# GpSimd's 128x512 tensor instructions of the mixing stages, issued as four of 128x128

## The chip, the cores and the metric

The kernel runs on one core of one Trainium2 chip. The metric is the device time of one execution in microseconds. Five engines of the core work side by side, each through its own instructions in order: TensorE (PE in the profile, with its weight loads as PEld), VectorE (DVE), ScalarE (ACT), GpSimd (POOL) and SyncE (SP), which here only issues DMAs. They wait for one another through semaphores.

## The reference: what is computed

A decoder trunk of two layers on a sequence of 512 positions with 1024 features, in float32. Each layer norms its input, projects it to the columns of three groups of heads, mixes them over the sequence, projects the mixture back, and adds a squared-ReLU MLP:

```python
for l in range(DEPTH):                                   # 2 layers
    h = rms_norm(x, norm_mix_g[l])
    p_att, p_conv, p_rwkv = jnp.split(h @ w_in[l], ...)
    o_att = diff_attention(...)      # 6 heads, causal
    o_conv = short_conv(...)         # 4 groups
    o_rwkv = rwkv7_time_mix(...)     # 6 heads, a recurrence over the sequence
    x = x + jnp.concatenate([o_att, o_conv, o_rwkv], axis=-1) @ w_out[l]
    h = rms_norm(x, norm_mlp_g[l])
    x = x + jnp.square(jax.nn.relu(h @ w_mlp_up[l])) @ w_mlp_down[l]
return rms_norm(x, final_norm_g)
```

## The kernel before, in words

Everything is held transposed: features on the 128 partitions, the 512 positions along the free axis, so that most tiles are 128x512. Each layer has a **mixing stage** (in the profiled execution about 16 to 298 us and 634 to 960 us) and an **MLP stage** (298 to 634 us and 960 to 1263 us).

A float32 product on TensorE is made of three passes: an operand is split into a rounded part (`whi`, `ahi`) and the rest (`wlo`, `alo`), and whi·ahi, whi·alo and wlo·ahi are added up in PSUM. Weights come in halves of four 128x128 tiles: SyncE loads `raw` (128x512, 256 KB), ScalarE casts it to `whi` (L687), and VectorE or GpSimd forms `wlo = raw - whi` (L699). A string of letters, `LO`, says for each half which of the two does it; `rests(dve)` and `rests(pool)` go through the list, and 62 of the halves are GpSimd's. There are three buffers each of `raw`, `whi` and `wlo`. `passes` then issues the three matmuls of one 128x128 weight tile, the wlo pass last.

In the mixing stage nothing is scheduled by a planner. Every job is a Python generator that yields after each instruction: `loads`, `casts`, `rests`, `products` (the projections `pj`, the output projection `po`, and the first three column groups of the MLP's up projection, `up`), `squares` and `inner_norm` (the MLP's norm), `rwkv_pair` and `rwkv_inverse` for each of three pairs of heads, `att_pair`, `conv` and others. A string `ORDER` of letters and counts, one string per layer, says which generator goes on next; `drive` walks through it. So the order in which each engine meets its instructions is written out by hand, and an engine that waits holds everything behind it.

GpSimd's 128x512 tensor instructions in the mixing stages are these, with their lines in the kernel before:

- L699 `wlo`, the rest of a weight half (62 times).
- L769 `accf`, the sum of the squares of x for the MLP's norm, in `norm_steps_of`, called by `squares` (7 per layer). Each adds `sqf`, ScalarE's square of one 128x512 tile of x (L766), to the sum; after the last, `inner_norm` has TensorE sum it over the partitions: four matmuls `pssf`, one per 128 positions (L290 is the helper that issues every matmul). On VectorE, `alof` (L756, in `inputs`) is formed at the same time for `up`.
- L942 `k`, L946 `bb` and L951 `bk` (once per pair of heads): three products in a row in `rwkv_pair`. `bk` and VectorE's `ar` (L950, L952) are the operands of the matmuls `pg`.
- L1016 the rest of a split operand, `pd..lo` (6 times in its several names).
- L1144 `nm` in `rwkv_inverse`: a masked copy, which VectorE reduces to `nd` (L1146). A DMA out and in turns it round, GpSimd inverts small triangles with 30 instructions of 64 partitions (L1158, L1160) and the result `xb` goes out and in by DMA (`dm` L1162, `xd` L1164) to VectorE's L1167 to L1186, and on to the matmuls `px`.
- L1184 `ee`, the other operand of `px`.
- L1248 `cz` and L1255 `cy` in `conv` (4 each).

Together they are 120 instructions. Three things on VectorE stand beside them: its own halves of `wlo` (L699), the operand rests `klo` and `qlo` of attention (L1273), and in `att_pair` the step from softmax sums to weights: `sm` (L1337, 128x1), then `pp` (L1339), then TensorE's transposes `ptt`.

GpSimd also has 128x512 subtractions `ml` in the MLP stages (L1405, 64 of them), a few 128x256 ones (L547), and instructions of the first norm (L400, L455); the change leaves them as they are.

Of the kernel before, what the change touches and what calls it, by code (L numbers as in the profile page):

```python
# [10 lines left out]
F32 = mybir.dt.float32  # L11
# [5 lines left out]
ALU = mybir.AluOpType  # L17
# [6 lines left out]
P = 128  # L24
NK = D // P
NB = S // P
C = 64
# [253 lines left out]
def tile_trunk(ctx: ExitStack, tc: tile.TileContext, xT, wts, prm_d, cst_d, lora_d, gup_d, lam_d, fin_d, out):  # L281
    nc = tc.nc
    act, dve, pool = nc.scalar, nc.vector, nc.gpsimd
# [44 lines left out]
    act.activation(cp.tile([P, NB], F32, tag="rr", bufs=2, name="rr0")[:, :1], ones1, AF.Sqrt)  # L328

    WB = 3  # L330
    lean = [False]

    def weights(g, k0=0, k1=NK, home=None):

        for a in range(k0, k1, 4):
            n = min(4, k1 - a)
            raw = wp.tile([P, 4, P], F32, tag="raw", bufs=WB, name=f"raw{g}_{a}")
            nc.sync.dma_start(raw[:, :n].rearrange("p k c -> p (k c)"), wts[g, :, a * P:(a + n) * P])
            if home is None:
                hi, lo = [wp.tile([P, 4, P], F32R, tag="w" + p, bufs=WB, name=f"w{p}{g}_{a}") for p in ("hi", "lo")]  # L340
            else:
# [47 lines left out]
    nrm = {}  # L389
# [198 lines left out]
    for l in range(L):  # L588
# [3 lines left out]
        key = f"m{l}"  # L592
        lean[0] = True
        with ExitStack() as mx:
# [37 lines left out]
            def loads():  # L632
# [8 lines left out]
                for kind, *o in order:  # L641
                    if kind == "w":
                        g, a, _, k0, k1 = o
                        if k0 == 0:
                            whole[g, a] = wp.tile([P, 4, P], F32, tag="raw", bufs=WB, name=f"raw{wbase + g}_{a}")
                        raw = raws[g, a, k0] = whole[g, a]
# [42 lines left out]
            def rests(which):  # L689
                whole = {}  # L690
                for i, (g, a, n, k0, k1) in enumerate(pieces):
                    eng = dve if g in head or LO[l][i - len(first)] == "x" else pool
                    if eng is which:
                        raw = yield from got(raws, (g, a, k0))
                        hi = yield from got(his, (g, a, k0))
                        if k0 == 0:
                            whole[g, a] = wtile(g, a, 1)
                        lo = los[g, a, k0] = whole[g, a]
                        yield eng.tensor_tensor(lo[:, k0:k1], raw[:, k0:k1], hi[:, k0:k1].bitcast(F32), ALU.subtract)  # L699

            def passes(out_ps, g, k, operand, first, last):
                at = piece(g, k)
# [55 lines left out]
            def norm_steps_of(j, key):  # L758

                if j == 0:  # L760
                    acc = wp.tile([P, S], F32, tag="acc", bufs=1, name=f"acc{key}")
                    nrm[key] = [acc]
                    yield act.activation(acc, x[j], AF.Square)
                else:
                    sq = wp.tile([P, S], F32, tag="sq", bufs=2, name=f"sq{key}_{j}")
                    yield act.activation(sq, x[j], AF.Square)  # L766
                    if j == NK - 1:
                        nrm["all" + key] = True
                    yield pool.tensor_tensor(nrm[key][0], nrm[key][0], sq, ALU.add)  # L769

            def inner_norm():
                key = f"f{l}"
# [122 lines left out]
            c3 = lambda ap: ap.rearrange("p (c s) -> p c s", s=C)  # L895
# [11 lines left out]
            m16 = cst[:, K_M16:K_M16 + C]  # L907
            B = 16

            def rwkv_pair(t):  # L910
                n = f"{l}_{t}"
                zk, zr = tmp(f"zk{t}"), tmp(f"zr{t}")
# [3 lines left out]
                sq = tmp(f"ksq{t}")  # L916
# [13 lines left out]
                w = yield from got(lw, t)  # L930
                dx = mp.tile([P, NCH, C + 1], F32, tag="dx", name=f"dx{n}")
                di = tmp(f"di{t}")
# [5 lines left out]
                a = yield from got(av, t)  # L938
                t1 = tmp(f"t1{t}")
                yield act.activation(t1, a, AF.Identity, scale=pr[:, C_KA + t:C_KA + t + 1], bias=dr[:, 11 + t:12 + t])  # L940
                k2 = tmp(f"k2{t}")
                yield pool.tensor_tensor(k2, zk, t1, ALU.mult)  # L942
                kkn = tmp(f"kkn{t}")
                yield act.activation(kkn, zk, AF.Identity, scale=kcol)
                bb = tmp(f"bb{t}")
                yield pool.tensor_tensor(bb, kkn, a, ALU.mult)  # L946

                ar = mp.tile([P, 2, NCH, C], F32, tag="ar", name=f"ar{n}")
                bk = mp.tile([P, 2, NCH, C], F32, tag="bk", name=f"bk{n}")
                yield dve.scalar_tensor_tensor(ar[:, 0], c3(kkn), -1.0, dx[:, :, :C], ALU.mult, ALU.mult)  # L950
                yield pool.tensor_tensor(bk[:, 0], c3(bb), c3(di), ALU.mult)  # L951
                yield dve.tensor_tensor(ar[:, 1], c3(zr), dx[:, :, 1:], ALU.mult)  # L952
                yield dve.tensor_tensor(bk[:, 1], c3(k2), c3(di), ALU.mult)

# [1 line left out]
                nn = mp.tile([P, 2 * NB, C], F32, tag="nn", name=f"nn{n}")  # L956
# [54 lines left out]
                pd = tmp(f"pd{t}")  # L1011
                yield dve.scalar_tensor_tensor(pd, zr, pr[:, C_RK + t:C_RK + t + 1], k2, ALU.mult, ALU.mult)
                phi = mp.tile([P, S], F32R, tag="ty", bufs=2, name=f"pd{n}hi")
                yield act.copy(phi, pd)
                plo = mp.tile([P, S], F32R, tag="ty", bufs=2, name=f"pd{n}lo")
                yield pool.tensor_tensor(plo, pd, phi.bitcast(F32), ALU.subtract)  # L1016
                zv = tmp(f"zv{t}")
                yield from shifted(21 + t, 6 + t, zv, f"v{t}")
                yield from got(ready, "exact")
# [7 lines left out]
                for b in range(NB):  # L1027
                    ins = pe.matmul(pt[:, b * P:(b + 1) * P], zv[:, b * P:(b + 1) * P], cent.bitcast(F32), start=True, stop=True)
# [5 lines left out]
                for b, h, q in QUADS:  # L1034
                    ins = pe.matmul(pbv[h][HF[q], b * C:(b + 1) * C], kq[X(h, q), b, h, 0], hd(vt, b, h, q), start=True, stop=True)
# [7 lines left out]
                for b, h, q in QUADS:  # L1043
                    ins = pe.matmul(pzw[h][X(h, q), b * P:(b + 1) * P], xi[HF[q], 2 * b + h],
                                    ab[HF[q], b, h].rearrange("p a s -> p (a s)"), start=True, stop=True)
# [7 lines left out]
                for b, h, q in QUADS:  # L1053
                    if (b, q) != (0, 0):
                        ins = pe.matmul(pap[q][HF[h], b * P:(b + 1) * P], zw[X(h, q), 2 * b + h, 0],
                                        bq[X(h, q), b, h].rearrange("p a s -> p (a s)"), start=True, stop=True)
                pbs = [psum("rp", 4, f"pbs{n}_{q}") for q in range(2)]
                for b in range(NB):
                    for part in range(2):
                        for h, q in ((0, 0), (1, 0), (1, 1), (0, 1)):  # L1060
                            if (b, q) != (NB - 1, 1):
                                l_, r_ = ((bq[X(h, q), b, h, 0], zw[X(h, q), 2 * b + h, 1]),
                                          (hd(kt, b, h, q), hd(vt, b, h, q)))[part]
                                ins = pe.matmul(pbs[q][HF[h], b * C:(b + 1) * C], l_, r_, start=(part == 0), stop=(part == 1))
# [40 lines left out]
                for c in range(1, NCH):  # L1105
                    q, at = c % 2, NB * C + c // 2 * C
                    for h in range(2):
                        ins = pe.matmul(pyy[h][HF[q], at:at + C], ptq[HF[h], c], state(c)[HF[h]], start=False, stop=True,
                                        skip_group_check=True)
# [29 lines left out]
            def rwkv_inverse(t):  # L1139

                n = f"{l}_{t}"
                nn = yield from got(ready, ("nn", t))
                nm = mp.tile([P, 2 * NB, C], F32, tag="ee", name=f"nm{n}")
                yield pool.tensor_tensor(nm, nn, m16.unsqueeze(1).to_broadcast([P, 2 * NB, C]), ALU.mult)  # L1144
                nd = mp.tile([P, 2 * NB, B], F32, tag="nd", name=f"nd{n}")
                yield dve.tensor_reduce(nd, nm.rearrange("p c (i s) -> p c s i", s=B), AX.X, ALU.add)  # L1146
                dn = dp.tile([NCH, P, B], F32, tag="dn", bufs=2, name=f"dn{n}")
# [33 lines left out]
                b3 = lambda ap: ap[:, :NB * C].rearrange("p (b s) -> p b s", s=C)  # L1181
                lv = cst[:, K_LV:K_LV + C].unsqueeze(1).to_broadcast([P, N8, C])
                ee = mp.tile([P, N8, C], F32, tag="ee", name=f"ee{n}")
                yield pool.tensor_tensor(ee, nn, lv, ALU.mult)  # L1184
                yi = mp.tile([P, N8, C], F32, tag="yi", name=f"yi{n}")
                yield dve.transpose(flat(yi), flat(x16))  # L1186
                px = [psum("rp", 4, f"px{n}_{h}") for h in range(2)]
                for b, h, q in QUADS:
                    i = 2 * b + h
                    ins = pe.matmul(px[h][X(h, q), b * C:(b + 1) * C], ee[HF[q], i], yi[HF[q], i], start=True, stop=True)  # L1190
# [5 lines left out]
                for b, h, q in QUADS:  # L1196
                    i = 2 * b + h
                    ins = pe.matmul(px2[h][HF[q], b * C:(b + 1) * C], rt[X(h, q), i], xs[X(h, q), b] if h else x16[HF[q], i],
                                    start=True, stop=True)
# [11 lines left out]
                for b, h, q in QUADS:  # L1211
                    i = 2 * b + h
                    ins = pe.matmul(px[h][UU[q ^ h][1], b * H:(b + 1) * H], nn[UU[q][0], i, H:], yj[UU[q][0], i, :H],
                                    start=True, stop=True)
# [8 lines left out]
                for b, h, q in QUADS:  # L1223
                    i, u = 2 * b + h, UU[q ^ h][1]
                    ins = pe.matmul(px2[h][UU[q][0], b * H:(b + 1) * H], rt2[u, i], xs[u, b, H:] if h else x16[u, i, H:],
                                    start=True, stop=True)
# [9 lines left out]
            def conv(i):  # L1236
                def part(g, name):
                    pt = yield from got(pjs, g)
                    rs = yield from got(ready, "rs")
                    r = tmp(f"{name}{i}", "tc", 2)  # L1240
                    yield dve.tensor_tensor(r, pt, rs, ALU.mult)
                    return r

                cc = yield from part(11 + i, "cc")
                uu = yield from part(13 + i, "uu")
                z = mp.tile([P, S + 2], F32, tag="cz", bufs=1, name=f"cz{l}_{i}")
                yield pool.memset(z[:, 0:2], 0.0)
                yield pool.tensor_tensor(z[:, 2:], cc, uu, ALU.mult)  # L1248
                bg = yield from part(9 + i, "bg")
                tap = lambda j: pr[:, C_CONV + 2 * j + i:C_CONV + 2 * j + i + 1]  # L1250
                y0 = tmp(f"cy{i}", "mix", MIX)
                yield act.activation(y0, z[:, 0:S], AF.Identity, scale=tap(0))
                yield dve.scalar_tensor_tensor(y0, z[:, 1:S + 1], tap(1), y0, ALU.mult, ALU.add)
                yield dve.scalar_tensor_tensor(y0, z[:, 2:S + 2], tap(2), y0, ALU.mult, ALU.add)
                yield pool.tensor_tensor(y0, y0, bg, ALU.mult)  # L1255
                yield from mix_out(3 + i, y0)


# [368 lines left out]
```

## Time and profile before

| | |
|---|---|
| time, median of 3 runs (lowest, highest) | 1266.44 us (1265.82, 1268.03) |
| the profiled execution's own time | 1265.12 us |
| its span in the trace | 1263.3 us |
| granted clock of TensorE, mean | 0.998 |
| PE busy | 1240.6 us, 98% of the span |
| DVE, ACT, POOL busy | 913.4, 697.7, 335.5 us (72%, 55%, 27%) |
| POOL busy in the two mixing stages | 114.2 us of 298, 127.5 us of 326 |
| GpSimd's 62 `wlo` instructions | 81.7 us, 1317 ns each |

The profile comes from one execution. Its times are starts and durations of instructions in microseconds; "idle before" is how long the engine stood still before an instruction, and the arrow names what ended that. A row of the timeline reads: start, duration, engine, line, operation, tile written <- tiles read, partitions x elements, and in brackets the idle time before it.

### The profile page before, as it was taken

What the parts mean: (1) busy time and instruction counts of PE and PEld (TensorE: products, weight loads), DVE (VectorE), ACT (ScalarE), POOL (GpSimd) and SP (SyncE); (2) the same over time, 40 slices, a digit from 0 to 9 for tenths busy, and PEclk for the clock granted to TensorE, in tenths of its full rate; (3) what the DMA queues carried; (4) which work ended last, traced back from release to release, by engine and by line L of the source; (5) the groups of instructions that cost most, each with busy time, mean ns of one, the idle gap of its engine ahead of it and who ended that gap; (6) DMA issues with size and microseconds to landing.
All of it is one profiled execution on the core that took longest, in us unless ns stands there. A gap on an engine that the chain in (4) does not pass through costs nothing.

```text
span 1263.3 us, 25161 instructions
## 1 busy us (share of the span) xinstructions
PE 1240.6 (98%) x9493; PEld 1049.3 (83%) x9493; DVE 913.4 (72%) x1894; ACT 697.7 (55%) x1479; POOL 335.5 (27%) x434
## 2 busy tenths in 40 slices
PE   9999999999999999999999999999999999999997
PEld 6777777787789898989878887887787989898987
DVE  6788888867976666765667787879598766666654
ACT  7675655646744544544475656564575545454553
POOL 1343526133300101010224345352431010111110
PEclk9999999999999999999999999999999999999999
DMA  6533333142343333321235334331434233333122
GB/s 212 159 85 94 109 94 101 52 133 84 100 126 101 101 101 100 101 84 51 75 103 146 98 102 110 98 97 60 133 93 133 92 109 95 107 99 102 59 75 76
DMA packets 84698, 127.93 MB, mean 101 GB/s; under 512 B 21472, under 2 KB 25568, under 8 KB 84576
## 3 DMA queue, kind: packets, MB, share of 16 engines
q1 hardware_dynamic: 83856, 125.77, 32.4%
q8 instruction: 75, 1.23, 0.4%
q10 hardware_dynamic: 720, 0.55, 0.1%
q14 instruction: 47, 0.39, 0.1%
HBM read 117.11 MB, written 9.18 MB: 100 GB/s over the span
## 4 chain that ended last, share of the span: by engine, by line
PE 71%; DVE 3%; ACT 1%; issue 1%; POOL 0%; POOLq 0%; DVEq 0%; ACTq 0%
PE dn L290 22%; PE pj L290 11%; PE pa L290 11%; PE pb L290 6%; PE up L290 6%; PE po L290 4%; PE dnF L290 3%; PE pc L290 3%; PE sc L290 1%; PE ptt L295 1%; PE pg L290 1%; DVE wlo L344 0%; DVE blo L1461 0%; DVE x L1537 0%; PE pyy L290 0%
## 5 line engine op out<-in xcount | busy, mean ns | idle before, releaser
L1405 POOL TENSOR_TENSOR ml<-m,mh 128x512 fp32r<-128x512 f32 x64 | 95.2, 1490 | 509.0 <-ACT mh L1404 490.8
L343 ACT CAST whi<-raw 128x512 fp32r<-128x512 f32 x142 | 88.0, 621 | 173.9 <-PE dn L290 158.2
L290 PE MATMUL dn<-mh,whi 128*128 128x512 f32 x448 | 175.4, 391 | 2.0 <-DVE x L1537 2.0
L290 PE MATMUL dn<-mh,wlo 128*128 128x512 f32 x448 | 174.7, 390 | 0.0
L290 PE MATMUL dn<-ml,whi 128*128 128x512 f32 x448 | 174.6, 390 | 0.0
L290 PE MATMUL pj<-ahim,whi 128*128 128x512 f32 x392 | 157.6, 402 | 4.4 <-DVE vf L1294 1.8
L290 PE MATMUL pj<-ahim,wlo 128*128 128x512 f32 x392 | 158.3, 404 | 0.0
L290 PE MATMUL pj<-alom,whi 128*128 128x512 f32 x392 | 158.2, 404 | 0.0
L687 ACT CAST whi<-raw 128x512 fp32r<-128x512 f32 x142 | 87.6, 618 | 93.3 <-PE pj L290 40.6
L699 POOL TENSOR_TENSOR wlo<-raw,whi 128x512 fp32r<-128x512 f32 x62 | 81.7, 1317 | 215.3 <-ACT whi L687 199.1
L1537 DVE TENSOR_TENSOR x<-dn,x 128x512 f32<-128x512 f32 x112 | 76.8, 686 | 76.7 <-PE dn L290 76.7
L344 DVE TENSOR_TENSOR wlo<-raw,whi 128x512 fp32r<-128x512 f32 x142 | 115.2, 811 | 11.3 <-ACT whi L343 10.7
L1476 DVE TENSOR_TENSOR slo_p<-s,shi_p 128x512 fp32r<-128x512 f32 x96 | 70.9, 741 | 63.5 <-ACT shi_p L1475 58.8
L290 PEld LDWEIGHTS dn<-mh,whi 128*128 128x128 f32 x448 | 84.1, 188 | 21.5 <-issue 2.4
L290 PEld LDWEIGHTS dn<-mh,wlo 128*128 128x128 f32 x448 | 84.1, 188 | 17.9
L290 PEld LDWEIGHTS dn<-ml,whi 128*128 128x128 f32 x448 | 84.1, 188 | 16.5
L290 PEld LDWEIGHTS pj<-ahim,whi 128*128 128x128 f32 x392 | 73.9, 188 | 19.9 <-issue 1.7
L1475 ACT CAST shi_p<-s 128x512 fp32r<-128x512 f32 x96 | 59.2, 617 | 49.7 <-PE pa L290 38.1
L290 PEld LDWEIGHTS pj<-ahim,wlo 128*128 128x128 f32 x392 | 73.8, 188 | 14.3 <-issue 0.9
L290 PEld LDWEIGHTS pj<-alom,whi 128*128 128x128 f32 x392 | 73.9, 188 | 14.0 <-issue 0.5
L290 PE MATMUL pa<-tlo,shi_p 128*128 128x256 f32 x288 | 81.4, 282 | 0.0
L290 PE MATMUL pa<-thi,shi_p 128*128 128x256 f32 x288 | 81.2, 282 | 0.0
(417 smaller groups left out, 3255.3 us busy)
## 6 DMA issues: line engine op xcount, KB each, us to landing
raw<-wts SPq DMA_DIRECT2D x389, 256.0 KB, 2.7
qs<-dqhi SPq DMA_DIRECT2D x24, 128.0 KB, 3.2
ks<-dkhi SPq DMA_DIRECT2D x24, 128.0 KB, 3.8
x<-xT SPq DMA_DIRECT2D x8, 256.0 KB, 4.5
dqhi<-qhi SPq DMA_DIRECT2D x6, 256.0 KB, 3.4
dqlo<-qlo SPq DMA_DIRECT2D x6, 256.0 KB, 3.0
dkhi<-khi SPq DMA_DIRECT2D x6, 256.0 KB, 2.7
dklo<-klo SPq DMA_DIRECT2D x6, 256.0 KB, 3.1
```

The lines of the kernel that those rows point to most:

```text
L290: ins = nc.tensor.matmul(*a, **k)
L295: ins = nc.tensor.transpose(*a, **k)
L343: act.copy(hi[:, :n], raw[:, :n])
L344: (pool if a and lean[0] else dve).tensor_tensor(lo[:, :n], raw[:, :n], hi[:, :n].bitcast(F32), ALU.subtract)
L687: yield act.copy(hi[:, k0:k1], raw[:, k0:k1])
L699: yield eng.tensor_tensor(lo[:, k0:k1], raw[:, k0:k1], hi[:, k0:k1].bitcast(F32), ALU.subtract)
L1405: pool.tensor_tensor(lo, m, hi.bitcast(F32), ALU.subtract)
L1475: act.copy(hi, src)
L1476: dve.tensor_tensor(lo, src, hi.bitcast(F32), ALU.subtract)
L1537: dve.tensor_tensor(x[j], pt, x[j], ALU.add)
```

## The change: what it does

A helper `pieced` issues a GpSimd tensor instruction on four quarters of the free axis, one after another: by the four weight tiles for `wlo` (whose tile has three axes), by blocks of 128 positions for the others, by chunks for those laid out as chunks. The generator still yields once, after the last quarter, so `ORDER` is unchanged. VectorE's share of `wlo` stays whole.

```diff
+    PARTS = 4
...
+    def pieced(out, a, b, op):
+
+        if len(out.shape) == 3 and out.shape[1] < PARTS:
+            n, cut = out.shape[1], lambda t, i: t[:, i:i + 1]
+        else:
+            n, w = PARTS, out.shape[1] // PARTS
+            cut = lambda t, i: t[:, i * w:(i + 1) * w]
+        for i in range(n):
+            ins = pool.tensor_tensor(cut(out, i), cut(a, i), cut(b, i), op)
+        return ins
...
-                        yield eng.tensor_tensor(lo[:, k0:k1], raw[:, k0:k1], hi[:, k0:k1].bitcast(F32), ALU.subtract)
+                        three = lo[:, k0:k1], raw[:, k0:k1], hi[:, k0:k1].bitcast(F32)
+                        yield pieced(*three, ALU.subtract) if eng is pool else dve.tensor_tensor(*three, ALU.subtract)
...
-                    yield pool.tensor_tensor(nrm[key][0], nrm[key][0], sq, ALU.add)
+                    yield pieced(nrm[key][0], nrm[key][0], sq, ALU.add)
...
-                yield pool.tensor_tensor(k2, zk, t1, ALU.mult)
+                yield pieced(k2, zk, t1, ALU.mult)
...
-                yield pool.tensor_tensor(bk[:, 0], c3(bb), c3(di), ALU.mult)
+                yield pieced(bk[:, 0], c3(bb), c3(di), ALU.mult)
```

The same replacement is made at `bb`, the rest of `pd`, `nm`, `ee`, `cz` and `cy`. The 120 instructions become 480, GpSimd has 360 more, and the sequences of the other engines stay as they were, but for their waits: where a reader takes one quarter, it now waits for that quarter.

GpSimd at the head of layer 1's first pair of heads, before (names: `dc` is a small copy, `k`, `bb`, `bk`, `nm` as above; the last numbers only tell buffers apart):

```order
L937 COPY dc_0_8177<-dx_0_8172 128x8 [waits Activation_49]
L942 TENSOR_TENSOR k_1_8190<-zk_1_8040,t_1_8180 128x512 [waits DVE_49,Activation_49]
L946 TENSOR_TENSOR bb_1_8206<-kkn_1_8193,av_0_8065 128x512 [waits Activation_49,Pool_49]
L951 TENSOR_TENSOR bk_0_8218<-bb_1_8206,di_1_8173 128x512 [waits DMAHW2_49,Pool_49]
L1144 TENSOR_TENSOR nm_0_8290<-nn_0_8239,cst 128x512 [waits DVE_49]
```

and the same place with the change (L342 is the helper's line):

```order
L950 COPY dc_0_8369<-dx_0_8364 128x8 [waits Activation_49]
L342 TENSOR_TENSOR k_1_8382<-zk_1_8229,t_1_8372 128x128 [waits DVE_49,Activation_49]
L342 TENSOR_TENSOR k_1_8382<-zk_1_8229,t_1_8372 128x128 x3
L342 TENSOR_TENSOR bb_1_8401<-kkn_1_8388,av_0_8254 128x128 [waits Activation_49,Pool_49]
L342 TENSOR_TENSOR bb_1_8401<-kkn_1_8388,av_0_8254 128x128 x3
L342 TENSOR_TENSOR bk_0_8416<-bb_1_8401,di_1_8365 128x128 [waits DMAHW2_49,Pool_49]
L342 TENSOR_TENSOR bk_0_8416<-bb_1_8401,di_1_8365 128x128 [waits Pool_49] x3
```

Nothing has moved: each row stands where it stood, four instructions deep, and the quarters of `bk` wait each for a quarter of `bb`.

TensorE behind them, at layer 1's first `pg` (64x64 tiles of `ar` and `bk`, block by block of 128 positions), before:

```order
L290 MATMUL pg_0_0_0_8242<-ar_0_8217,bk_0_8218 64x128 [waits DVE_49,Pool_49]
L290 MATMUL pg_0_0_1_8243<-ar_0_8217,bk_0_8218 64x64 x4
L290 MATMUL pg_0_0_0_8242<-ar_0_8217,bk_0_8218 64x128 x2
L290 MATMUL pg_0_0_1_8243<-ar_0_8217,bk_0_8218 64x64 x4
L290 MATMUL pg_0_0_0_8242<-ar_0_8217,bk_0_8218 64x128 x2
```

and with the change:

```order
L290 MATMUL pg_0_0_0_8443<-ar_0_8415,bk_0_8416 64x128 [waits DVE_49,Pool_49]
L290 MATMUL pg_0_0_1_8444<-ar_0_8415,bk_0_8416 64x64 x4
L290 MATMUL pg_0_0_0_8443<-ar_0_8415,bk_0_8416 64x128
L290 MATMUL pg_0_0_0_8443<-ar_0_8415,bk_0_8416 64x128 [waits Pool_49]
L290 MATMUL pg_0_0_1_8444<-ar_0_8415,bk_0_8416 64x64 x4
```

The sequence is the same; a wait on GpSimd has been added at the first matmul of each further block. In the same way the three later `pssf` matmuls each wait for their own quarter of `accf`, and each wlo pass for its own weight tile.

More of the change, by code (lines that the diff above doesn't have):

```diff
@@ L945, in rwkv_pair @@
                 bb = tmp(f"bb{t}")
-                yield pool.tensor_tensor(bb, kkn, a, ALU.mult)
+                yield pieced(bb, kkn, a, ALU.mult)
                 ar = mp.tile([P, 2, NCH, C], F32, tag="ar", name=f"ar{n}")
@@ L1015, in rwkv_pair @@
                 plo = mp.tile([P, S], F32R, tag="ty", bufs=2, name=f"pd{n}lo")
-                yield pool.tensor_tensor(plo, pd, phi.bitcast(F32), ALU.subtract)
+                yield pieced(plo, pd, phi.bitcast(F32), ALU.subtract)
                 zv = tmp(f"zv{t}")
@@ L1143, in rwkv_inverse @@
                 nm = mp.tile([P, 2 * NB, C], F32, tag="ee", name=f"nm{n}")
-                yield pool.tensor_tensor(nm, nn, m16.unsqueeze(1).to_broadcast([P, 2 * NB, C]), ALU.mult)
+                yield pieced(nm, nn, m16.unsqueeze(1).to_broadcast([P, 2 * NB, C]), ALU.mult)
                 nd = mp.tile([P, 2 * NB, B], F32, tag="nd", name=f"nd{n}")
@@ L1183, in rwkv_inverse @@
                 ee = mp.tile([P, N8, C], F32, tag="ee", name=f"ee{n}")
-                yield pool.tensor_tensor(ee, nn, lv, ALU.mult)
+                yield pieced(ee, nn, lv, ALU.mult)
                 yi = mp.tile([P, N8, C], F32, tag="yi", name=f"yi{n}")
@@ L1247, in conv @@
                 yield pool.memset(z[:, 0:2], 0.0)
-                yield pool.tensor_tensor(z[:, 2:], cc, uu, ALU.mult)
+                yield pieced(z[:, 2:], cc, uu, ALU.mult)
                 bg = yield from part(9 + i, "bg")
@@ L1254, in conv @@
                 yield dve.scalar_tensor_tensor(y0, z[:, 2:S + 2], tap(2), y0, ALU.mult, ALU.add)
-                yield pool.tensor_tensor(y0, y0, bg, ALU.mult)
+                yield pieced(y0, y0, bg, ALU.mult)
                 yield from mix_out(3 + i, y0)
```

## The prediction

> **What bounds the kernel now.** I read the busy shares first, then the chain that ended last, then what TensorE waits for, and only then GpSimd's own rows. From the page, the busy time of each engine and the shares of the chain that ended last:
>
> ```profile
> PE 1240.6 (98%) x9493; PEld 1049.3 (83%) x9493; DVE 913.4 (72%) x1894; ACT 697.7 (55%) x1479; POOL 335.5 (27%) x434
> PE 71%; DVE 3%; ACT 1%; issue 1%; POOL 0%; POOLq 0%; DVEq 0%; ACTq 0%
> ```
>
> TensorE works 98% of the span, so only some 23 us (1263.3 - 1240.6) are idle; that is about all a better order of the others could win. GpSimd has no share of the chain worth printing. What TensorE waits for (us in total, times, longest):
>
> ```profile
> PE ptt L295 <- DVE pp L1339: 2.8, 4, 0.9
> PE pj L290 <- DVE vf L1294: 1.8, 2, 0.9
> PE pj L290 <- DVE pg L812: 1.1, 1, 1.1
> PE pj L290 <- DVE pk L812: 0.7, 1, 0.7
> PE pssf L290 <- POOL accf L769: 0.2, 1, 0.2
> ```
>
> The one wait on GpSimd is 0.2 us; the largest, and 3.6 us of further ones (1.8 + 1.1 + 0.7), are on VectorE. So handing TensorE a quarter earlier has almost nothing to save; what the change can move is how long GpSimd takes in all, and how it and VectorE get in each other's way.
>
> **What a quarter costs.** GpSimd's groups by shape (busy us, mean ns of one), then two instructions that follow each other without a wait:
>
> ```profile
> L699 POOL TENSOR_TENSOR wlo<-raw,whi 128x512 fp32r<-128x512 f32 x62 | 81.7, 1317 | 215.3 <-ACT whi L687 199.1 <-PE pj L290 7.7 <-DVE mlo L880 2.7
> L547 POOL TENSOR_TENSOR o<-x,rbs 128x256 f32<-128x256 f32 x4 | 2.9, 736 | 45.0 <-ACT rbs L542 45.0
> ...
> 277.47 1.30 POOL L699 TENSOR_TENSOR wlo<-raw,whi 128x512 fp32r<-128x512 f32 x1
> 278.72 1.29 POOL L769 TENSOR_TENSOR accf<-accf,sqf 128x512 f32<-128x512 f32 x1
> ```
>
> No 128x128 tensor_tensor is in the trace. An undisturbed 128x512 takes 1.29 us, a 128x256 0.736: 256 columns are 0.554 us, the fixed part is 0.182, and a quarter comes to 0.182 + 0.277 = 0.46 us, an estimate. Successive instructions start 1.25 apart at a duration of 1.30, so 0.05 overlaps: four quarters take 0.46 + 3 x 0.41 = 1.69 us, **0.40 more** than one whole; 120 of them, 48 us of GpSimd's time. The lower bound is four quarters at 1.29 / 4 (fixed part hidden), no gain or loss; the upper is four times 0.46 with no overlap, 0.55 more.
>
> The Trainium skill, "GPSIMD Engine Reference", section "2.1 Instruction dispatch", says that consecutive Pool instructions are no barrier between the eight Q7 cores: a core starts the next one when its own share is done. By that rule much of the fixed part could hide behind the neighbour, and the 0.40 go towards zero; the pair above, which overlaps by 0.05 us, speaks for only a little of that, and the sum goes by the pair.
>
> **GpSimd and VectorE exclude each other.** From the timeline, VectorE operations beside GpSimd ones:
>
> ```profile
> 71.05 1.27 POOL L699 TENSOR_TENSOR wlo<-raw,whi 128x512 fp32r<-128x512 f32 x1
> 71.18 1.69 DVE L817 SCALAR_TENSOR_TENSOR zv<-pv,prm,dv 128x512 f32<-128x512 f32 x1
> 72.29 0.69 POOL L1158 TENSOR_TENSOR tt<-nb,xb 64x39 f32<-64x39 f32 x1
> 73.06 0.26 POOL L1160 TENSOR_TENSOR xb<-xb,tt 64x39 f32<-64x39 f32 x1
> ...
> 159.34 0.68 DVE L880 TENSOR_TENSOR mlo<-yc,mhi 128x512 fp32r<-128x512 f32 x1
> ...
> 943.12 3.95 POOL L1405 TENSOR_TENSOR ml<-m,mh 128x512 fp32r<-128x512 f32 x1 [5.19 <-ACT mh L1404]
> ```
>
> A VectorE operation on two 128x512 inputs from SBUF takes 0.68 us; `zv`, begun at 71.18 under a `wlo`, has not ended until 72.87, as if it began when the `wlo` ended. The next small GpSimd instruction, started at 72.29, then takes 0.69 where the next of its size, at 73.06, takes 0.26: at GpSimd's boundary the waiting VectorE operation goes first. At 943 one GpSimd instruction stretches to 3.95 us, 2.66 over its 1.29, while VectorE's operations follow one another. So a cut of one GpSimd instruction into four makes three boundaries: VectorE gets in earlier, and each time it does, GpSimd's remaining quarters come some 0.68 us later.
>
> **The terms.** (1) *The norm's sum*, the end of each mixing stage. Timeline of layer 0, then of layer 1:
>
> ```profile
> 289.67 1.32 POOL L769 TENSOR_TENSOR accf<-accf,sqf 128x512 f32<-128x512 f32 x1 [1.55 <-ACT sqf L766]
> 290.18 1.37 DVE L756 SCALAR_TENSOR_TENSOR alof<-x,prm,ahif 128x512 fp32r<-128x512 f32 x1 [0.33 <-ACT ahif L755]
> 291.05 1.05 PE L290 MATMUL pssf<-ones,accf 128*128 128x1 f32 x8 [0.16 <-POOL accf L769]
> 291.46 0.68 DVE L699 TENSOR_TENSOR wlo<-raw,whi 128x512 fp32r<-128x512 f32 x1
> 291.96 0.48 PE L290 MATMUL up<-alof,whi 128*128 128x512 f32 x1
> ...
> 910.53 1.32 POOL L769 TENSOR_TENSOR accf<-accf,sqf 128x512 f32<-128x512 f32 x1 [1.71 <-ACT sqf L766]
> 911.91 1.05 PE L290 MATMUL pssf<-ones,accf 128*128 128x1 f32 x8
> ```
>
> `pssf` starts as the last `accf` ends. In quarters, `accf` ends at 289.67 + 1.69 = 291.36 if nothing gets in, at 292.05 after one VectorE operation and 292.7 after two (`alof`, ready at 290.18, and the `wlo` behind it both stand there); I take 292.4. The eight `pssf` steps, two to a quarter, take 1.05, 0.13 each, so the last quarter's pair was due at 291.05 + 6 x 0.13 = 291.8: +0.6 us, bounds 0 and 0.9. `up<-alof`, 0.4 us behind its `alof`, is next in TensorE's order and `alof` now stands behind quarters that themselves come later: +0.4 more. Together 1.0 per layer, the same in both: **+2.0** (0 to 3).
>
> (2) *k, bb, bk, pg*, six times. Timeline at layer 1's first pair, and the end of the chain at layer 0's second:
>
> ```profile
> 669.24 1.30 POOL L942 TENSOR_TENSOR k<-zk,t 128x512 f32<-128x512 f32 x1 [1.05 <-ACT t L940]
> 670.62 1.62 POOL L946 TENSOR_TENSOR bb<-kkn,av 128x512 f32<-128x512 f32 x1
> 672.32 1.62 POOL L951 TENSOR_TENSOR bk<-bb,di 128x512 f32<-128x512 f32 x1
> 674.41 0.68 DVE L953 TENSOR_TENSOR bk<-k,di 128x512 f32<-128x512 f32 x1
> 674.90 1.24 PE L290 MATMUL pg<-ar,bk 64*64 64x128 f32 x48
> ...
> 118.21 1.29 POOL L951 TENSOR_TENSOR bk<-bb,di 128x512 f32<-128x512 f32 x1
> 120.75 0.63 PE L290 MATMUL pg<-ar,bk 64*64 64x128 f32 x20
> ```
>
> `bk` ends at 673.94, 0.96 before `pg` starts. The chain grows by 3 x 0.40 = 1.2, and VectorE, which today gets in once between two wholes, may get in between quarters: one to two times more, 0.7 to 1.4. Less the slack of 0.96, and less the part of `pg`'s 1.24 us that passes before its last block: 1.2 + 1.0 + 0.4 (the later start of VectorE's own half of `bk`, behind GpSimd's quarters) - 0.9 = +1.7. At layer 0's second pair the slack is 1.25 (119.50 to 120.75), just the chain's growth without a slip; I take the other five for like it, 0.4 for all of them. **+2.1** (0 to 6).
>
> (3) *The inverses.* `nd`, `dm`, `xd` and `px` follow GpSimd's `nm` and small instructions, between which stand `wlo`'s. With `nm` and three `wlo` in the way, `xb` comes 4 x 0.40 = 1.6 us later. The timeline of layer 0's second pair, and what the weight loads of all `px` stood idle for:
>
> ```profile
> 155.85 0.71 DVE L1186 STREAM_TRANSPOSE yi<-x 128x512 f32<-128x512 f32 x1
> 158.08 0.65 PE L290 MATMUL px<-yi,ee 64*64 64x64 f32 x32
>   issue: 1.1, 3
> ```
>
> Here `yi` ends at 156.56, 1.5 before `px`: covered. Three of six show a wait before `px`; were it `yi` each time, 3 x 1.3 = 3.9. I take one: **+1.3** (0 to 3.9).
>
> (4) *The gain.* Where VectorE's 128x1 `sm` meets a whole GpSimd instruction, it takes 1.26 us (at 84.90) instead of 0.22 (at 152.86), and TensorE waits for `pp` behind it:
>
> ```profile
> 84.87 1.28 POOL L1184 TENSOR_TENSOR ee<-nn,cst 128x512 f32<-128x512 f32 x1
> 84.90 1.26 DVE L1337 SCALAR_TENSOR_TENSOR sm<-s0q,nlam,sm 128x1 f32<-128x1 f32 x1
> 86.61 0.33 PE L295 MATMUL ptt<-cst,pp 128*128 128x128 f32 x1 [0.86 <-DVE pp L1339]
> ...
> 152.86 0.22 DVE L1337 SCALAR_TENSOR_TENSOR sm<-s0q,nlam,sm 128x1 f32<-128x1 f32 x1
> ...
> 211.29 0.55 PE L295 MATMUL ptt<-cst,pp 128*128 128x128 f32 x3 [0.60 <-DVE pp L1339]
> ...
> 855.69 0.33 PE L295 MATMUL ptt<-cst,pp 128*128 128x128 f32 x1 [0.78 <-DVE pp L1339]
> ```
>
> With quarters `sm` gets in after the first, about 0.46 - 0.03 + 0.22 = 0.65 after its start at 84.90, at least 0.6 us sooner than today; nearly all of 0.86 + 0.60 + 0.78 = 2.24 goes: **-2.2** (-2.3 to 0).
>
> (5) *Everything else on VectorE.* GpSimd's 48 us raise its 335.5 by a seventh, so VectorE meets it a seventh more often, for a shorter time each. On the 3.6 us of VectorE waits above this is +0.5 by frequency alone; bounds -1.8 (half of them gone with the shorter holds) and +2.4 (each of the four grown by 0.6).
>
> The 62 `wlo` themselves I cost at nothing on TensorE. Their consumers come later by more than the 0.40, and the first quarter of each comes sooner, which the wlo pass behind it can use; only SyncE's loads, which wait for the buffer, shift by 0.40, and they stand ahead of the casts by more than that (GpSimd waits 199.1 of its 215.3 idle us before `wlo` for ScalarE's cast, not the reverse). Uncovered, 62 x 0.40 would be 25 us, which the idle rows exclude.
>
> The sum: 2.0 + 2.1 + 1.3 - 2.2 + 0.5 = **+3.7 us**. The profiled execution took 1265.12 us, 1.8 more than its span and 1.3 less than the median of 1266.44; on the median the forecast is **1270.1 us**.
>
> The Trainium skill, "Perfetto Trace Analysis", section "Optimizing Scalar/DVE Operations", says that where engines which aren't saturated cause bubbles on others, breaking up their instructions may let work complete sooner. The 0.2 us of TensorE's waiting on GpSimd leave that rule next to nothing here, apart from the 2.2 us of term 4; by the rule alone the time would be 1264.2.
>
> **Rivals.** *Faster.* If the quarters run at a pace of 1.29 / 4 = 0.32, terms 1 to 3 vanish, the ptt waits go (-2.2) and the shorter holds take up to 1 us off the VectorE waits: 1263.2. It decides where the measured start-to-start of quarters is below about 0.35. Against it stand the 736 ns of the half-size instruction. 0.12.
>
> *Starved GpSimd, slower still.* Where VectorE has back-to-back work, every boundary lets it in. The 943 row shows 2.66 us lost to one run. Were it 2 us at each of the six k-bb-bk chains past their slack, 1266.4 + 12 = 1278. For it: `bb` and `bk` show 1.62 where 1.29 is free, so VectorE is dense there. Against: the slack of five of six. 0.18.
>
> *No change.* The late results (1) to (3) shrink by slack that I don't see, to 2 or 3 us, and meet term 4: 1266.4. 0.20.
>
> That the change doesn't do what it says is excluded by the order: four rows stand for each one, and the readers wait for theirs.
>
> **The numbers.** The forecast, slower by a few us, has 0.50. A measurement can tell about 0.2%, 2.5 us, from no change; so faster 0.12, same 0.20, slower 0.50 + 0.18 = 0.68. The range, 1263.5 to 1278, takes in the cases of all signs but the ends of the first two; the forecast's own is 1267.5 to 1274.
>
> **What would show it.** Quarters of 0.46 us starting 0.41 apart, so POOL near 384 us busy (335.5 + 48). `sm` at 84.9, 209.3 and 853.9 at 0.7 or less, with the ptt waits gone. `pssf` waiting 0.5 us or more on `accf`; `pg` at 675 later by 1.5 or more against its neighbours. If quarters start 0.33 apart, or `pssf` and `pg` wait no longer than before, the forecast is wrong towards faster; if GpSimd's chains grow by more than 3 us each, towards slower.

## The result, and the profile after

The changed kernel takes **1278.42 us** (median of 4, 1276.19 to 1279.67) against 1266.85 us (the kernel before, now over 4 executions): ratio 1.0096, 95% interval 1.0084 to 1.0108, or 11.6 us more. The direction was forecast; the size was not (1270.1), and the time lies 0.4 us above the range. The profiled execution took 1278.56 us, with a span of 1276.8 us, 13.5 more than the one of before.

The same parts of the page as before the change, busy time and the chain that ended last, then what TensorE waits for, and GpSimd's groups by shape:

```profile
PE 1249.3 (98%) x9493; PEld 1054.1 (83%) x9493; DVE 914.3 (72%) x1894; ACT 698.3 (55%) x1479; POOL 400.5 (31%) x794
PE 69%; DVE 3%; POOL 2%; ACT 1%; issue 1%; POOLq 0%; DVEq 0%; ACTq 0%
```

```profile
PE pssf L290 <- POOL accf L342: 2.7, 6, 0.5
PE ptt L295 <- DVE pp L1352: 1.6, 3, 0.8
PE pg L290 <- POOL bk L342: 1.3, 1, 1.3
```

```profile
L342 POOL TENSOR_TENSOR wlo<-raw,whi 128x128 fp32r<-128x128 f32 x248 | 111.1, 479 | 190.3 <-ACT whi L699 175.5 <-PE pj L290 7.0 <-issue 2.5
L342 POOL TENSOR_TENSOR accf<-accf,sqf 128x128 f32<-128x128 f32 x56 | 30.5, 578 | 5.8 <-ACT sqf L779 5.8
L342 POOL TENSOR_TENSOR bb<-kkn,av 128x128 f32<-128x128 f32 x24 | 13.6, 600 | 0.4
```

GpSimd is busy 65 us longer (400.5 - 335.5), and it now has a share of the chain. TensorE waits 4.0 us for it (2.7 + 1.3) where it waited 0.2. But TensorE itself is also *busy* 8.7 us longer (1249.3 - 1240.6) with the same 9493 matmuls, so part of the loss is in no wait at all. Somewhat over half of these 8.7 us (4.7, worked out below) is in the clock; the rest was not traced. Three pairs of stretches of 3.4 us of the change, one right behind the other, then one pair of before at layer 1's first norm (after the two ends and the length: PE busy, PEld, DVE, ACT, POOL, then the granted clock, DMA share, GB/s):

```profile
294.87:298.28 3.41, 2.43 (x12) 2.05 (x13) 3.28 (x6) 1.81 (x3) 1.69 (x2) 0.99 0.21 77
298.28:301.69 3.41, 3.41 (x9) 2.63 (x9) 0.16 (x1) 1.20 (x2) 0.52 (x2) 0.51 0.29 82
...
642.97:646.38 3.41, 2.43 (x15) 1.84 (x15) 1.89 (x5) 1.38 (x4) 3.41 (x7) 1.00 0.28 96
646.38:649.80 3.42, 3.42 (x12) 2.83 (x11) 0.71 (x4) 0.62 (x1) 1.21 (x3) 0.50 0.88 303
922.87:926.28 3.41, 2.33 (x12) 1.95 (x13) 3.04 (x5) 1.06 (x2) 1.79 (x3) 1.00 0.29 82
926.28:929.69 3.41, 3.41 (x10) 2.64 (x9) 0.50 (x1) 1.13 (x2) 0.00 (x0) 0.50 0.23 77
```

```profile
637.32:640.74 3.42, 2.59 (x16) 1.97 (x15) 1.94 (x7) 0.91 (x3) 1.99 (x2) 1.00 0.84 275
640.74:644.15 3.41, 3.41 (x21) 2.95 (x20) 0.87 (x3) 1.52 (x4) 2.06 (x4) 1.00 0.37 130
```

In the change there are three places where TensorE was less busy for 3.4 us and the clock stood at a half for the next 3.4. Before, the same norm kept 1.00. TensorE's matmuls under it, in the change:

```profile
297.87 0.39 PE L290 MATMUL up<-ahif,wlo 128*128 128x512 f32 x1
298.09 0.51 PE L290 MATMUL up<-ahif,whi 128*128 128x512 f32 x1
...
299.25 0.63 PE L290 MATMUL up<-ahif,whi 128*128 128x512 f32 x1
299.68 0.63 PE L290 MATMUL up<-alof,whi 128*128 128x512 f32 x1
```

Starts lie 0.43 us apart instead of 0.22, so 3.41 us bring the work of about 1.75, and each such stretch costs some **1.6 us**.

TensorE's sequence is the same in both kernels, so the start of the same weight load can be compared. The lag, by how much later the change starts it (us), at places along the span of before:

| place | lag | what lies between |
|---|---|---|
| 19 us | +0.76 | the first loads (other runs with nothing changed there show +0.45) |
| 84 us, before the first ptt wait | +2.61 | layer 0's first pair |
| 87 us, after it | +1.62 | the wait gone |
| 118 us | +2.59 | given back at the next ptt |
| 288 us, before pssf | +3.58 | rest of layer 0, second ptt wait gone |
| 293.4, 301 us | +4.57, +6.11 | pssf, then the half clock |
| 639, 648 us | +6.18, +7.79 | layer 1's first norm, half clock |
| 673, 678 us | +7.78, +9.60 | layer 1's first pg |
| 908 us | +9.77 | rest of layer 1, third ptt wait gone |
| 914, 919 us | +11.91, +13.49 | pssf, then the half clock |
| 1257 us | +13.46 | MLP |

Of the 13.5, then, 4.7 are three half-clock stretches (1.54 + 1.61 + 1.58), 3.1 the two pssf, 1.8 the one pg, 0.8 the start, and 3.1 what is left of the rest after the gains.

At the end of layer 0, where the profile of before showed one accf of 1.32 us:

```profile
293.25 3.31 POOL L342 TENSOR_TENSOR accf<-accf,sqf 128x128 f32<-128x128 f32 x4 [0.17 <-ACT sqf L779]
294.48 0.78 PE L290 MATMUL pssf<-ones,accf 128*128 128x1 f32 x4
295.73 0.38 PE L290 MATMUL pssf<-ones,accf 128*128 128x1 f32 x2 [0.48 <-POOL accf L342]
296.61 0.38 PE L290 MATMUL pssf<-ones,accf 128*128 128x1 f32 x2 [0.50 <-POOL accf L342]
```

Four quarters take 3.31 us, since VectorE gets in at every boundary. This accf starts where it did before (289.67 us and the lag of 3.58 make 293.25); what is late is its end. At layer 1 it is different:

```profile
914.74 1.72 POOL L342 TENSOR_TENSOR wlo<-raw,whi 128x128 fp32r<-128x128 f32 x4
916.42 8.24 POOL L342 TENSOR_TENSOR accf<-accf,sqf 128x128 f32<-128x128 f32 x12
```

Twelve quarters stand here without a pause, and the last accf starts at 921.15, 1.0 us after its square was ready: GpSimd is behind. Over both layers, accf has stood idle 5.8 us for its squares; it stood 15.6 before.

### The profile page after: what moved, and what is told of

Read it like the earlier page. It is cut to its first block, busy times and chain, and to the rows that moved or that the text cites. A ratio compares the mean times of both kernels' runs of the same rounds, so it can differ in the third digit from the quotient of the medians.

```text
span 1276.8 us, 25553 instructions
## 1 busy us (share of the span) xinstructions
PE 1249.3 (98%) x9493; PEld 1054.1 (83%) x9493; DVE 914.3 (72%) x1894; ACT 698.3 (55%) x1479; POOL 400.5 (31%) x794
## 4 chain that ended last, share of the span: by engine, by line
PE 69%; DVE 3%; POOL 2%; ACT 1%; issue 1%; POOLq 0%; DVEq 0%; ACTq 0%
PE dn L290 22%; PE pa L290 11%; PE pj L290 10%; PE up L290 6%; PE pb L290 5%; PE po L290 3%; PE dnF L290 3%; PE pc L290 3%; POOL accf L342 1%; PE sc L290 1%; PE ptt L295 1%; PE pg L290 1%; DVE wlo L356 0%; DVE x L1550 0%; DVE blo L1474 0%
## 5 line engine op out<-in xcount | busy, mean ns | idle before, releaser
L342 POOL TENSOR_TENSOR wlo<-raw,whi 128x128 fp32r<-128x128 f32 x248 | 111.1, 479 | 190.3 <-ACT whi L699 175.5
```

Of the source, the lines that this page charges most:

```text
L342: ins = pool.tensor_tensor(cut(out, i), cut(a, i), cut(b, i), op)
```

## The experiments

**Theory:** GpSimd's results come too late, in part because a quarter costs more and in part because VectorE gets in between quarters, and the lateness falls on the two norms (and one pg), where it also takes TensorE's activity under what keeps the clock up. **Rivals:** the lateness alone is the cost and the clock a coincidence; each instruction pays its part wherever it stands; the added waits of TensorE cost by themselves. Most kernels quarter only a part, through one more argument of the helper:

```diff
-    def pieced(out, a, b, op):
+    def pieced(out, a, b, op, kind):
+        if kind not in SPLIT:
+            return pool.tensor_tensor(out, a, b, op)
```

**Each group alone.** `SPLIT = ("accf",)`:

> Only the 14 accf instructions in quarters, all else whole. Theory A (late norm sum plus clock): pssf comes 1 to 2 us late in each layer, and the granted clock falls to a half for some 3.4 us behind it, 1.5 us each: +5 to +7 us, about 1273. Theory B (lateness alone): the same pssf delay and a full clock: +2 to +4, about 1270.

1265.98 us against 1265.39, ratio 1.0003 (0.9994 to 1.0012): **both theories missed**. The pssf of each layer is about 0.4 us late by the lag, and the clock stays full.

```profile
289.24 2.63 POOL L345 TENSOR_TENSOR accf<-accf,sqf 128x128 f32<-128x128 f32 x4 [1.05 <-ACT sqf L782]
...
910.42 2.64 POOL L345 TENSOR_TENSOR accf<-accf,sqf 128x128 f32<-128x128 f32 x4 [1.27 <-ACT sqf L782]
```

The last accf still waits 1.05 and 1.27 us for its square: GpSimd is not behind, and VectorE gets in twice, not three times. From here on the texts speak of a backlog theory: only where accf and what stands between in GpSimd's order are all in quarters does GpSimd go from one to the next without a pause and fall behind.

`SPLIT` all but `"accf"`:

> All in quarters except accf. Theory A: the clock stays full behind pssf (298 and 926 us), the rest of the 11.6 us remains: +5 to +6 us, about 1272. Theory B (lateness summed over all instructions, accf's 14 of 120 being no more than the others): +9 or more, about 1276.

1270.53 us, ratio 1.0039 (1.0027 to 1.0052), +5.1. The clock at both pssf is full, as theory A had it; layer 1's first norm had its half clock in the profiled execution (1.6 us by the lag).

`SPLIT = ("wlo",)` and `SPLIT = ("bb", "bk", "k")`:

> Only the 62 wlo in quarters. If wlo is covered as the prediction has it, within 1 us of before; if GpSimd's 25 us more of wlo push its other results late, +2 to +4 us.

> Only k, bb and bk in quarters. By the trace of the change, layer 1's first pg comes 1.4 to 1.8 us late and the other five 0.3 or less each: +2 to +3 us, as the prediction had it. If the chains feed on lateness from elsewhere, under +1.

wlo: 1266.13 us, ratio 1.0004 (0.9995 to 1.0013), +0.7, as the covered case has it. By the lag of the profiled execution (+1.5) this is a balance: 1.6 us are lost to a half clock at layer 1's first norm and 0.8 gained at the third ptt wait, beside smaller pieces. Two wlo stand at that norm. The first of them before the change, then in quarters, and the stretch behind it:

```profile
635.36 1.44 POOL L699 TENSOR_TENSOR wlo<-raw,whi 128x512 fp32r<-128x512 f32 x1 [3.01 <-ACT whi L687]
635.57 2.76 POOL L345 TENSOR_TENSOR wlo<-raw,whi 128x128 fp32r<-128x128 f32 x4 [3.02 <-ACT whi L702]
640.36:643.77 3.41, 3.41 (x11) 2.78 (x10) 0.73 (x4) 0.68 (x2) 1.11 (x4) 0.50 0.90 284
```

The half clock at this norm stands in the profiles of five of the six kernels with all wlo in quarters, and of none of the eight others. So it goes with wlo; by which wait was not tried.

k-bb-bk: 1267.43 us, ratio 1.0012 (1.0003 to 1.0020), +2.0, as expected; all of it lies at layer 1's first pg, by the lag -0.53 before it and +1.29 after it:

```profile
671.44 3.40 POOL L345 TENSOR_TENSOR bb<-kkn,av 128x128 f32<-128x128 f32 x4
671.84 0.95 DVE L969 TENSOR_TENSOR bk<-k,di 128x512 f32<-128x512 f32 x1
674.80 2.14 POOL L345 TENSOR_TENSOR bk<-bb,di 128x128 f32<-128x128 f32 x4
675.75 1.56 PE L290 MATMUL pg<-ar,bk 64*64 64x128 f32 x38 [1.31 <-POOL bk L345]
```

Here quarters and VectorE's operations take turns: four quarters of bb take 3.40 us, and a VectorE operation 0.95 instead of 0.68.

`SPLIT = ("cy", "cz", "ee", "nm", "pd")`, and later these with `"wlo"`:

> Only pd, nm, ee, cz and cy in quarters. wlo, accf and k-bb-bk alone came to +0.7, +0.6 and +2.0 us. If the terms add up, the rest must be the +1.8 that is left of all but accf (5.1 - 0.7 - 2.0 = 2.4 at most). If the instructions only cost together, it is within 0.7 like the others.

> wlo and the rest (pd, nm, ee, cz, cy) in quarters, accf and k-bb-bk whole. Alone they cost +0.7 and +0.9. If they add up: +1.6, and all but accf (+5.1) then has 1.5 us that belongs to k-bb-bk with the others. Backlog theory: wlo and the rest share GpSimd with the small instructions of the inverses at 64 to 84 us, and together cost +3 to +4 there, with k-bb-bk adding its own +2.

The rest alone: 1266.56 us, ratio 1.0008 (0.9999 to 1.0017), +0.9, between its two cases. With wlo: 1267.55 us, ratio 1.0015 (1.0006 to 1.0024), +2.3, also between its two. That is near the sum of the two (1.7), and with k-bb-bk's 2.0 it leaves 0.8 of all but accf, about what these medians can tell. So as long as accf is whole, the groups about add up.

**The norm.** With accf they don't: 0.6 alone, 6.5 on top of all others (11.6 - 5.1). `SPLIT = ("accf", "wlo")`:

> accf and wlo in quarters, the rest whole. Alone they cost +0.6 and +0.7. If terms add up: +1.3, about 1267. Backlog theory: at the end of a stage GpSimd has wlo and accf in turn, and only with both in quarters does it fall behind: pssf 2 us late in layer 1, two half-clock stretches, +5 to +7.

1272.35 us against 1265.63, ratio 1.0049 (1.0037 to 1.0062), **+6.7**: as the backlog theory had it, not the sum. The five executions are one of 1268.72 us at a mean clock of 0.997, and four of 1271.72 to 1273.43 at 0.993 or 0.994. So the lateness alone is some 3 us and the half clock some 4 more; where the four had it was not profiled. GpSimd and one VectorE instruction in the one of 1268.72, which was profiled and has no half clock in its stages:

```profile
899.61 1.74 POOL L345 TENSOR_TENSOR wlo<-raw,whi 128x128 fp32r<-128x128 f32 x4
901.29 3.40 POOL L345 TENSOR_TENSOR accf<-accf,sqf 128x128 f32<-128x128 f32 x8
904.63 1.72 POOL L345 TENSOR_TENSOR wlo<-raw,whi 128x128 fp32r<-128x128 f32 x4
908.39 7.77 POOL L345 TENSOR_TENSOR accf<-accf,sqf 128x128 f32<-128x128 f32 x12 [2.04 <-ACT sqf L782]
...
901.27 5.63 DVE L715 TENSOR_TENSOR wlo<-raw,whi 128x512 fp32r<-128x512 f32 x1
```

The row at 908.39 is one way it goes: twelve quarters that would take 5.0 us (0.46 + 11 x 0.41) take 7.77, with VectorE in between. The row at 901.27 is the other: a VectorE operation of 0.68 us stands for 5.63 us, through twelve quarters in a row, and TensorE's `po` waits 1.6 us for what is behind it (1.8 by the lag). The last accf itself is 0.3 us behind its square here, and its pssf adds 1.3; layer 0's adds 1.1. So what the two groups do together, in this execution, is to keep GpSimd at it without a pause, and to hold VectorE or let it in at a bad place.

**Lateness without quarters.** All whole, one more instruction ahead of the last accf:

```diff
+                    if j == NK - 1:
+                        pool.tensor_tensor(sq, sq, ones1.to_broadcast([P, S]), ALU.mult)
                     yield pool.tensor_tensor(nrm[key][0], nrm[key][0], sq, ALU.add)
```

> All whole as before; one more whole 128x512 GpSimd instruction (sqf times one) ahead of the last accf of each layer. It makes pssf about 1.3 us late without any quarter. Clock theory: the 3.4 us stretch around pssf falls under the share of activity at which the clock halves, in most executions: +1.3 and +1.5 per layer, +4 to +6 us. Lateness alone: +2.6.

1270.72 us against 1265.63, ratio 1.0038 (1.0026 to 1.0051), **+5.1**. The fastest execution, with the highest mean clock (0.997), took 1268.25 us: +2.6, what was expected of the lateness alone. It was not the profiled one, which is this:

```profile
293.99 1.13 PE L290 MATMUL pssf<-ones,accf 128*128 128x1 f32 x8 [1.56 <-POOL accf L771]
```

```profile
291.42:294.83 3.41, 1.85 (x13) 1.37 (x11) 3.13 (x3) 2.71 (x5) 2.44 (x2) 1.00 0.00 0
294.83:298.25 3.42, 3.42 (x10) 2.74 (x11) 2.32 (x5) 0.00 (x0) 0.00 (x0) 0.50 0.28 86
```

Layer 1 shows the same pair, and by the lag each pssf with its half clock costs 2.8 us. (This profile has a third half clock at 18 us, in the first loads, where nothing was changed; it has nothing to do with pssf.) So a pssf that is late makes the half clock, whether or not anything is cut; the rival of coincidence falls.

**The last four quarters.** The whole change with the last accf of each layer whole:

```diff
+        met[kind] = met.get(kind, -1) + 1
+        if (kind, met[kind]) in (("accf", 6), ("accf", 13)):
+            return pool.tensor_tensor(out, a, b, op)
```

> The whole change, but the last accf of each layer whole. If the last four quarters with VectorE's operations between them are what makes pssf late, the time falls to that of all but accf, +5 to +6. If the backlog from the earlier quarters is enough, GpSimd starts the last one late anyhow: +8 to +10, with half-clock stretches left in some.

1275.74 us against 1265.77, ratio 1.0078 (1.0065 to 1.0092), +10.0: most of the loss stays, but in one layer only. Layer 0's last accf, and VectorE ahead of layer 1's:

```profile
292.56 1.52 POOL L338 TENSOR_TENSOR accf<-accf,sqf 128x512 f32<-128x512 f32 x1 [0.18 <-ACT sqf L783]
...
907.99 5.63 DVE L716 TENSOR_TENSOR wlo<-raw,whi 128x512 fp32r<-128x512 f32 x1
```

At layer 0, pssf and what follows cost 0.3 us by the lag (2.88 to 3.17) at a full clock, where the whole change loses 2.5: there the last four quarters, stretched by VectorE, were the cost. At layer 1 the loss is 4.2 (6.89 to 11.08), where the whole change loses 3.7. Of it, 1.8 come ahead of the norm, where VectorE is held for 5.63 us as in the run with accf and wlo; the rest is a late pssf and its half clock. There the lateness is made before the last accf, and TensorE's added waits for its quarters aren't the cost.

**Halves.** `PARTS = 2` for all 120:

> The whole change with two halves instead of four quarters. A half takes 0.74 us, two some 1.43, so 0.13 more than whole instead of 0.41, and VectorE meets one boundary instead of three. Backlog theory: GpSimd keeps up, no half-clock stretch behind pssf: +1 to +3 us. If the quartering of readiness were the cost (the added waits of TensorE), a half of the change's 11.6 or so.

1265.36 us against 1265.77, ratio 1.0000 (0.9992 to 1.0009): **nothing lost**, less than was expected. GpSimd's groups:

```profile
L342 POOL TENSOR_TENSOR wlo<-raw,whi 128x256 fp32r<-128x256 f32 x124 | 91.1, 755 | 205.4 <-ACT whi L699 192.3 <-PE pj L290 7.4 <-DVE mlo L893 2.5
L342 POOL TENSOR_TENSOR accf<-accf,sqf 128x256 f32<-128x256 f32 x28 | 21.5, 789 | 12.5 <-ACT sqf L779 12.5
```

accf stands idle 12.5 us for its squares (15.6 before, 5.8 in quarters): GpSimd keeps up, and no half clock stands in the stages. TensorE has added waits here too, one for each instruction in place of three, and they cost nothing that shows. Whether it is the smaller price of a cut or the two boundaries less that saves the 11.6 us was not separated.

**The gain by itself.** Only the instructions under which `sm` was held, three and then two of them:

```diff
+    SPLIT = {("ee", 0), ("cy", 0), ("wlo", 53)}
```

> Only the three instructions under which sm was held are in quarters: the first ee, the first cy and the wlo at 853.9. By the prediction's term 4 the three ptt waits go: -2.0 us or a little less. If a waiting VectorE operation is held through all four quarters, the waits stay or grow: 0 to +1.

1264.83 us against 1265.63, ratio 0.9996 (0.9987 to 1.0005), between its two cases. Two of the three ptt waits went, 0.85 and 0.87 by the lag; at the third the hold grew:

```profile
84.44 1.70 POOL L347 TENSOR_TENSOR ee<-nn,cst 128x128 f32<-128x128 f32 x4
84.48 1.68 DVE L1355 SCALAR_TENSOR_TENSOR sm<-s0q,nlam,sm 128x1 f32<-128x1 f32 x1
...
86.60 0.33 PE L295 MATMUL ptt<-cst,pp 128*128 128x128 f32 x1 [1.29 <-DVE pp L1357]
```

`sm` did not get in after a quarter; it was held through all four, 1.68 us, and TensorE waited 1.29 instead of 0.86. Without that one (`SPLIT = {("cy", 0), ("wlo", 53)}`):

> Only two instructions in quarters, the first cy and the wlo at 853.9, where GpSimd stands idle ahead of the first quarter and sm got in after it in the run before. Each takes 0.85 us off TensorE's wait: -1.7 us on an execution, -1.2 to -1.7 on the median. If what is saved is given back downstream, 0.

**1263.88 us** against 1265.77, ratio 0.9986 (0.9977 to 0.9995): 1.9 us faster, the best of all these kernels.

```profile
209.51 2.16 POOL L347 TENSOR_TENSOR cy<-cy,bg 128x128 f32<-128x128 f32 x4 [0.74 <-DVE sm L1353]
209.54 0.44 DVE L1355 SCALAR_TENSOR_TENSOR sm<-s0q,nlam,sm 128x1 f32<-128x1 f32 x1
```

## Why the prediction failed, step by step

- **The price of a quarter** held: 0.46 us, four in 1.70 to 1.72 against 1.69, so 0.40 more than a whole. The rule of the Trainium skill that was weighed beside it ("GPSIMD Engine Reference", section "2.1 Instruction dispatch") could have hidden much of the fixed part; of the 0.18 us, only the 0.04 to 0.05 by which neighbours overlap were hidden. GpSimd's busy time rose by 65 us, not 48. Most of the other 17 lie in accf (6.7), k-bb-bk (4.9) and wlo (4.6), by their busy time less 0.40 for each cut: the rows that VectorE's turns stretch, like bb's 3.40 us.
- **"At GpSimd's boundary the waiting VectorE operation goes first"** failed as a rule. It held at accf and k-bb-bk, and in each case that I looked at where GpSimd had stood idle ahead of its first quarter. Wherever, in the kept traces, VectorE was held over more than one further quarter, GpSimd had come to the first quarter straight from another instruction (though VectorE also got in at some of those). What decides there stays open. The change itself shows where a gain of term 4 went:

```profile
87.77 1.71 POOL L342 TENSOR_TENSOR ee<-nn,cst 128x128 f32<-128x128 f32 x4
88.08 1.94 DVE L830 SCALAR_TENSOR_TENSOR zk<-pk,prm,dk 128x512 f32<-128x512 f32 x1
...
92.58 0.44 PE L295 MATMUL ptt<-cst,pp 128*128 128x128 f32 x2 [0.77 <-DVE pp L1352]
```

  `sm` passed ahead of ee there and the first ptt wait shrank, but `zk` was held through all four quarters (1.94 us where it took 0.74), and the next ptt lost the 0.98 us again.
- **Term 1** was the step that failed most, by what it left out. Its mechanism, pssf behind a cut accf with VectorE in between, is what happened, and at layer 0 its size was right: 1.0 us forecast, 1.0 by the lag (3.58 to 4.57). At layer 1 it was 2.1, not 1.0, since the working looked at the last accf alone, while GpSimd came to it 1.0 us late from a row of quarters of accf *and* wlo (0.6 and 0.7 alone, 6.7 together). And it had no term for the clock: a late pssf halves it for 3.4 us, 1.6 us each time, 3.1 us in the profile at the two pssf. A third half clock, 1.6 us at the first norm of layer 1, is in no term either. These 4.7 us of clock and the 1.1 us at layer 1's pssf are over half of what the forecast lacks of the 13.5 us (9.8).
- **Term 2** had the right size in the right place: +2.0 us for k-bb-bk alone (forecast 2.1), 1.8 of it at the pg that was named. Part of that is luck. The working names two things to take off, the slack of 0.96 and the part of `pg` ahead of its last block, and takes off only one 0.9. And GpSimd's `bk` ended not 2.2 us later but 3.5 (676.93 in that run, 673.94 before, lag -0.53), since VectorE took turns with most of the quarters. The two errors go against each other.
- **Term 3 and term 5** together were put at 1.8 us. In the profiled execution of the rest with wlo, losses away from the half clock (1.6 us) come to some 3.2 by the lag, beside what the ptt waits gave: too small by some 1.4 us. Which wait of the inverses each belongs to was not tried.
- **Term 4** was right for two of its three places (forecast 0.60 + 0.78, by the lag 0.85 + 0.87, measured 1.9) and of the wrong sign at the third.
- **"The 62 wlo I cost at nothing"**: +0.7, not told from nothing, by themselves; but they are a half of the backlog at the norm of layer 1's end, and at that layer's first norm the half clock came only with all wlo in quarters.
- **The rivals.** The starved GpSimd, at 0.18, came nearest in its time (1278), but its price was put at six k-bb-bk chains, of which one paid; the time came from elsewhere, so its nearness is luck. The rule of the Trainium skill, "Perfetto Trace Analysis", section "Optimizing Scalar/DVE Operations", that breaking up instructions may let work complete sooner (said there of ScalarE and VectorE), proves right for the two instructions of the last run above (1.9 us faster) and wrong for the 120.

## What to carry to other kernels

Cutting an instruction pays at the place where its hold on another engine is waited for, and costs wherever the engine that issues it has a due time; so cut the two that were waited for, not the kind. On an engine that is 40% busy in a stage, look for the stretch in which it is fully busy, and for the places where another engine takes turns with it: there the 0.4 us per instruction did not vanish. And where the bounding engine waits, ask what the wait does to its clock: with one more whole instruction, a wait of 1.6 us in place of 0.2 cost 2.8.

## What the runs showed of the hardware

The half clock lasts 3.41 us, once, and follows 3.41 us of low activity. Counting TensorE's time in matmuls other than the 128x1 ones (each from its start to the next start, at most 0.24 us), the stretches ahead of a half clock within the stages show a share of 0.25 to 0.41, and the lowest without one 0.41 to 0.42: all but accf at 640.0 us has 0.412 and a half clock, halves at 637.4 has 0.414 and none, before at 637.3 has 0.420 and none. If the 128x1 ones are counted like the others, the two sets overlap (up to 0.68 with a half clock, down to 0.45 without), so they count for little or nothing. The kernel before stands within a hundredth of the edge at layer 1's first norm, so that little is needed there. The Trainium skill, "TensorE: Matmul & The Clock Gate", section "🔬 Part 1: The HAM clock gate (the "warmup" mystery)", tells of a free-running window of 3413 ns after whose idleness the clock is halved; the length agrees, but "idle" here begins at 0.41 of the window, with no gap between matmuls longer than 1.6 us in it (all but accf at 640.0 us: 1.9 us if the 128x1 ones count as a gap).

VectorE operations on two SBUF inputs and GpSimd's tensor instructions took turns or held one another whole in every row shown. The Trainium skill, "SBUF — State Buffer", section "🔬 SBUF: two separate sides", calls this an exclusive lock for a whole instruction; the rows agree, and add that instructions issued back to back can keep it from one to the next, through twelve of them and 5.63 us.
